# Opening the two fixed expert rounds of a mixture-of-experts layer by halves of the channels

## Chip, core and metric

The kernel runs on one NeuronCore of a Trainium2 chip. Its engines each work through a list of instructions of their own and wait for each other through semaphores: TensorE (PE; its weight loads are shown as PEld), VectorE (DVE), ScalarE (ACT), GpSimd (POOL) and SyncE (SP), which here only issues the transfers of weights. The metric is the device time of one execution in microseconds (us); lower is better.

## What is computed

A decoder trunk of two layers for 512 tokens of 1024 channels. Each layer has a token mixer (attention, gating unit, convolution), an output projection with layer norm, and a mixture of 32 experts of which each token uses two. The part that matters here is the experts:

```python
g_logit = xt @ wg + bg ; e_logit = xt @ we + be          # 4 groups, 8 experts in each
_, g_idx = lax.top_k(g_logit, 1)                         # one group,
top_logit, top_local = lax.top_k(e_logit_of_group, 2)    # two experts inside it
expert = g_idx * EXPERTS_PER_GROUP + top_local
...
def run_block(args):                                     # tokens of one expert
    rows, e = args
    xb = x_pad[rows]                                     # the gather
    hdn = jax.nn.silu(xb @ w_gate[e]) * (xb @ w_up[e])
    return hdn @ w_down[e]
...
out = segment_sum(y_rows[dest] * gate_sorted, tok_sorted)
x = layer_norm(ALPHA * x + out, ...)
```

All 32 experts are read in every layer: three matrices of 2 MB each, 6 MB per expert, 192 MB per layer in float32.

## The kernel before

**Rounds.** Each layer handles its experts in 13 rounds (`NR`). Rounds 0 and 1 (`FIXED`, `R0 = 2`) serve two experts each that are named in the program, so that their weights can be fetched before the router has decided; each of these experts has room for 64 tokens. Rounds 2 to 12 serve two or three experts each, chosen at run time: the experts are sorted by how many tokens they got, and the order (`self.ids`) is read by SP into registers that address the transfers. A round gathers its tokens (a product with a one-hot matrix), multiplies by the gate and up matrices (`first`, `hidden`, L1374), forms silu(gate) x up (`act`, L1386 and L1387), turns it (`turn`, L1393), multiplies by the down matrix (`second`, L1405), scales by the token's weight (`gated`) and adds the rows back to the tokens (`spread`, L1423).

**Gather.** `gather(quarters, n)` does a quarter of the channels at a time, two blocks `k` of 128 channels each. For each block eight matmuls add up: four 128-token blocks times a high part (`x1h`, fp32r) and a low part (`x1l`, f16). The moving operand is the one-hot matrix `oh` (in `fa`) or its f16 copy `oh16`, with 128 columns per round. `n=2` gathers for two rounds at once, so 256 columns. The result in a PSUM bank `t` is copied to `xg` (in the tile `f`) by ACT for the even block (L1345) and by DVE for the odd one (L1343); the DVE copy waits for the ACT copy.

**Weights.** Weight tiles of 1 MB (`w`) go into buffers from one free list (`self.free`). `feed` issues a transfer for each free buffer in the order of `self.queue`: all gate and up tiles of both fixed rounds (16), their eight down tiles, and then the tiles of the rounds chosen at run time. When the experts' part begins, the 16 gate and up tiles and one down tile are in place, and no buffer is free. A transfer therefore waits until the last product that reads the old tile in its buffer is done. SP issues strictly in order: a transfer that waits holds up all behind it. `hidden` with `parts=((0, 4), (4, 8))` does the gate products of channel blocks 0 to 3, the up products of 0 to 3, then gate and up of 4 to 7, so that the first half of the gate tiles comes free first.

**Order around the change.** PE, DVE, ACT, POOL and SP stand in written order here (`manual`). PE ends the router with six matmuls on the identity (`warm`, L1116) and then does: gather quarter 0, the sort's counting products (`sort_a`, L1213), gather quarter 1, the sort's table product (`sort_b`, L1226, which waits for four DVE operations L1221 to L1225), gather quarters 2 and 3, and then all gate and up products of round 0, with two `by_slot` transposes (L1356) in between and behind. DVE does the copies of the gather, the sort's few operations, the tokens' weights (`gating`, `gating_all`, `tokens`, L1249 to L1285), and the one-hots for rounds 2 and 3 (`gates`, L1306 to L1312).

Of the kernel before, what the change touches and what calls it, by code (L numbers as in the profile page):

```python
# [15 lines left out]
AF = mybir.ActivationFunctionType  # L16
# [149 lines left out]
class Trunk:  # L166
# [702 lines left out]
    def output(self, l):  # L869
# [118 lines left out]
        with self.manual(ET.PE):  # L988
# [31 lines left out]
            self.oh16 = f[:, 5, :].bitcast(F16).rearrange("p (a t s) -> p a t s", a=2, t=NT)  # L1020
            self.count_up()
            self.rank(NT - 1)
            self.places()
            self.warm(6)
            for r in range(R0):
                self.onehots(r)
            self.keys()
        self.give(wltag)
# [79 lines left out]
        nc.tensor.matmul(ps[:, 0:36], lt, self.two, start=False, stop=True)  # L1108
        nc.vector.tensor_copy(self.L[:, t, :], ps[:, 0:36])

    def warm(self, n):

        if n:
            ps = self.g()
        for _ in range(n):
            self.nc.tensor.matmul(ps[:, 0:128], self.ident, self.ident, start=True, stop=True)  # L1116

    def choose(self, tiles, more=()):

# [66 lines left out]
        ab, rk = self.ab[:, a:b, :], self.rk[:, a:b, :]  # L1186
        self.nc.vector.scalar_tensor_tensor(rk, ps, 1.0, ab, OP.add, OP.mult)

    def places(self):

        v = self.nc.vector
        self.ranks(NT - 1, NT)
        for r, (a, b) in enumerate(FIXED):
            le, on = (self.rt[:, c : c + 8].rearrange("p (t e) -> p t e", t=NT) for c in (384, 392))
            rk, u = self.rk[:, :, a : b + 1 : b - a], self.u[:, r, :]
            v.scalar_tensor_tensor(le, rk, 64.0, rk, OP.is_le, OP.mult)
            v.tensor_scalar(on[:, :, 0], le[:, :, 1], 0.0, 64.0, OP.is_gt, OP.mult)
            v.tensor_tensor(u, le[:, :, 0], le[:, :, 1], OP.add)
            v.tensor_tensor(u, u, on[:, :, 0], OP.add)


    def keys(self):
# [112 lines left out]
    def moe(self, l):  # L1315
# [5 lines left out]

        gain, bias = (lambda k, c=c: self.pp[:, c + k : c + k + 1] for c in (34, 42))

        def gather(quarters=range(4), n=2):

            w = 128 * n
            for kk in quarters:
                ps = self.t()
                for j in range(2):
                    k = 2 * kk + j  # L1330
                    i = 0
                    for src, one in ((x1h, oh), (x1l, self.oh16)):
                        for t in range(NT):
                            nc.tensor.matmul(  # L1334
                                ps[:, w * j : w * j + w], src[:, k, 128 * t : 128 * t + 128],
                                one[:, 0:n, t, :], start=(i == 0), stop=(i == 2 * NT - 1),
                            )
                            i += 1
                for j in range(2):
                    k = 2 * kk + j  # L1340
                    src = ps[:, w * j : w * j + w]
                    if j:
                        nc.vector.tensor_scalar(xg[:, k, 0:w], src, gain(k), bias(k), OP.mult, OP.add)  # L1343
                    else:
                        nc.scalar.activation(xg[:, k, 0:w], src, AF.Identity, bias=bias(k), scale=gain(k))  # L1345

        def gate_of(r):
            return self.sm.tile([128, 1], F32, tag="gv", name="gv")
# [16 lines left out]
        def weights(r, *names):  # L1365
            return [self.loaded[(l, n, r, e)] for n in names for e in range(members(r))]
# [179 lines left out]
        def release(r, *names):  # L1546
            for n in names:
                self.drop(*((l, n, r, e) for e in range(members(r))))

        def first(r, fill=(), keep=0):  # L1550

            pss = [self.g(), self.g()]
            xs = xg[:, :, 128 * (r % 2) : 128 * (r % 2) + 128]
            if r >= R0:
                for m, n in enumerate(("gate", "up")):
                    if m:
                        self.feed()
                    hidden(pss[m:], [weights(r, n)], xs, columns(ROUNDS[r - R0]), fill[4 * m : 4 * m + 4])
                    release(r, n)
            else:  # L1560
                w = [weights(r, n) for n in ("gate", "up")]
                hidden(pss, w, xs, halves, fill, ((0, 4), (4, 8)))
                release(r, "gate", "up")
            if keep == 1:
                spare.append(self.free.pop())
            held = [self.free.pop() for _ in range(4 if keep == 4 else 0)]
            self.feed()
            self.free.extend(held)
            return pss
# [22 lines left out]
        spare, row_steps = [], []  # L1592
        with self.manual(ET.PE, ET.SP):

            gather((0,))
            self.sort_a()
            gather((1,))
            self.sort_b()
            gather((2,))
            self.sort_c()  # L1600
            self.known = l
            self.feed()
            gather((3,))
            self.gating()
            self.gating_all()
            for r in range(R0):
# [2 lines left out]
                    in1=self.Gp[:, r, :].unsqueeze(2).broadcast_to([128, NT, 128]), op=OP.mult,  # L1609
                )  # L1610
            self.tokens()
            slots = []
            none = lambda: None
            pss = first(0, [none] * 5 + [lambda: slots.append(by_slot(0)), none, lambda: slots.append(by_slot(1))])
            h = act(pss)
            self.gates(2)
            self.gates(3)
            self.counts()
            nc.gpsimd.tensor_copy(self.cnt[:, 64:96], self.perm)
            pss = first(1, [none, lambda: turn(h, hT)])  # L1620
            self.fb = self.half("y", FR, "Y")[0]
            oT, gv = slots[0]
            steps = spreads(0, oT, second(0, gv))
# [228 lines left out]
```

## Time and profile before

| what | value |
|---|---|
| time, median of 3 runs | 1521.49 us (1520.38 to 1523.6) |
| the profiled execution | 1520.52 us; its span 1518.8 us |
| PE busy | 1368.6 us (90%) |
| DVE / ACT / POOL busy | 683.3 us (45%) / 397.2 us (26%) / 156.0 us (10%) |
| moved by DMA | 445.16 MB, mean 293 GB/s over the span |

The span is the stretch from the first to the last instruction in the trace; the execution's own time is 1.72 us longer. Busy shares are means over stages with different limits. The page's 40 slices show DMA at 410 to 419 GB/s in two long stretches, which are the experts' part of either layer, and between 1 and 56 GB/s just ahead of them. The experts' part of layer 0 begins at about 268 us of the span, that of layer 1 at about 1026 us.

### The profile page before, as it was taken

The numbers are of one execution on the slowest core, as the hardware profiler recorded it, in microseconds if no ns is written. First come the engines' busy times: TensorE is split into PE (matmuls) and PEld (weight loads), VectorE is DVE, ScalarE is ACT, GpSimd is POOL, SyncE is SP. The second block draws the span as 40 slices with busy tenths as digits, with TensorE's granted clock in tenths as the row PEclk, the third lists the DMA queues.
The fourth block names the chain that finished last, engine by engine and source line by source line (L and its number), as shares of the span: only waits on it lengthen the run. The fifth ranks groups of instructions, "written<-read, shape, count | busy, mean of one in ns | idle before, by whom it ended". The sixth has DMA issues, their size and how long they took to land. (4 is left out here: it accounts for less than half of the span.)

```text
span 1518.8 us, 22582 instructions
## 1 busy us (share of the span) xinstructions
PE 1368.6 (90%) x8828; PEld 750.3 (49%) x8829; DVE 683.3 (45%) x1528; ACT 397.2 (26%) x720; POOL 156.0 (10%) x190
## 2 busy tenths in 40 slices
PE   8999997999989898989699998979999898989894
PEld 7776576443434342434377665864434343433341
DVE  4347758534242424232553676585352424241325
ACT  5446544110101010101463555341101010101013
POOL 2112206000000000000141221060000000000001
PEclk9999999899999998999799998999999999999997
DMA  9410354499999999999911025444999999999994
GB/s 346 141 56 1 113 193 166 164 411 408 419 419 419 418 419 410 419 418 410 382 45 59 1 84 192 141 167 184 410 410 419 419 418 419 419 410 419 419 404 151
DMA packets 84551, 445.16 MB, mean 293 GB/s; under 512 B 8080, under 2 KB 14352, under 8 KB 36816
## 3 DMA queue, kind: packets, MB, share of 16 engines
q1 hardware_dynamic: 83184, 440.15, 72.2%
q0 software_dynamic: 960, 2.90, 0.6%
q8 instruction: 74, 1.21, 0.3%
q10 hardware_dynamic: 288, 0.52, 0.1%
q14 instruction: 45, 0.37, 0.1%
HBM read 441.45 MB, written 2.10 MB: 292 GB/s over the span
## 5 line engine op out<-in xcount | busy, mean ns | idle before, releaser
L1374 PE MATMUL g<-w,f 128*32 128x512 f32 (+1 forms) x3072 | 411.8, 602 | 36.3 <-DMA w<-expert_w_up 26.9
L1374 PEld LDWEIGHTS g<-w,f 128*32 128x32 f32 (+1 forms) x3072 | 113.6, 113 | 303.5 <-issue 220.6
L1405 PE MATMUL g<-w,f 128*32 128x512 f32 (+1 forms) x1536 | 215.4, 642 | 31.3 <-DMA w<-expert_w_down 15.6
L1405 PEld LDWEIGHTS g<-w,f 128*32 128x32 f32 (+1 forms) x1536 | 58.8, 118 | 165.0 <-issue 125.3
L1416 DVE SCALAR_TENSOR_TENSOR y<-g,gv,y 128x512 fp32r<-128x512 f32 x52 | 39.1, 751 | 208.8 <-ACT y L1415 206.4
L1428 DVE TENSOR_TENSOR X<-X,s 128x512 f32<-128x512 f32 x88 | 56.4, 683 | 127.1 <-PE s L1423 127.1
L1415 ACT ACTIVATE y<-g,gv 128x512 fp32r<-128x512 f32 x52 | 35.8, 689 | 245.0 <-PE g L1405 245.0
L1334 PE MATMUL t<-fa,mh 128*128 128x256 f32 (+1 forms) x448 | 82.8, 308 | 0.6 <-DVE f L1207 0.6
L1387 DVE TENSOR_TENSOR f<-g,f 128x512 f32<-128x512 f32 x26 | 17.9, 690 | 134.3 <-PE g L1374 130.9
L1345 ACT ACTIVATE f<-t,pp 128x256 f32<-128x256 f32 (+1 forms) x56 | 30.9, 551 | 177.1 <-PE t L1334 177.1
L1343 DVE TENSOR_SCALAR f<-t,pp 128x256 f32<-128x256 f32 (+1 forms) x56 | 29.4, 525 | 90.8 <-ACT f L1345 90.8
L1334 PEld LDWEIGHTS t<-fa,mh 128*128 128x128 f32 x448 | 62.7, 197 | 12.4 <-DVE X L1428 8.4
L1334 PE MATMUL t<-f,x1l 128*128 128x256 f16 (+1 forms) x448 | 67.5, 275 | 0.0
L1428 DVE TENSOR_TENSOR X<-X,t 128x512 f32<-128x512 f32 x88 | 56.3, 682 | 19.9 <-PE t L1423 19.9
L1423 PE MATMUL s<-y,fa 128*128 128x512 f32 x208 | 62.8, 422 | 2.4 <-ACT y L1415 1.8
L1386 ACT ACTIVATE f<-g 128x512 f32<-128x512 f32 x26 | 15.6, 598 | 188.3 <-PE g L1374 188.3
L1534 POOL DMA_DIRECT2D rows<-ln_gain x2 | 1.1, 550 | 586.9 <-PEq L1450 586.9
L1423 PEld LDWEIGHTS s<-y,fa 128*128 128x128 f32 x208 | 35.0, 188 | 51.2 <-issue 40.1
L1423 PE MATMUL t<-y,fa 128*128 128x512 f32 x208 | 59.1, 405 | 0.5 <-DVE xl L462 0.5
L1394 ACT COPY f<-s 128x512 f32<-128x512 f32 x26 | 15.2, 587 | 162.9 <-PE s L1393 135.1
L409 POOL TENSOR_TENSOR X<-X,E 128x512 f32<-128x512 f32 x11 | 16.3, 1486 | 332.5 <-ACT X L1712 168.8
L409 POOL TENSOR_TENSOR X<-X,f 128x512 f32<-128x512 f32 x32 | 40.9, 1309 | 87.8 <-DVE x1l L953 82.3
(343 smaller groups left out, 2273.8 us busy)
## 6 DMA issues: line engine op xcount, KB each, us to landing
w<-expert_w_gate SPq DMA_DIRECT2D x128, 1024.0 KB, 19.8
w<-expert_w_up SPq DMA_DIRECT2D x128, 1024.0 KB, 19.8
w<-expert_w_down SPq DMA_DIRECT2D x116, 1024.0 KB, 19.8
w<-w_in SPq DMA_DIRECT2D x20, 1024.0 KB, 13.9
w<-expert_w_down SPq DMA_DIRECT2D x48, 256.0 KB, 5.4
w<-w_out SPq DMA_DIRECT2D x8, 1024.0 KB, 5.5
X<-x SPq DMA_DIRECT2D x4, 512.0 KB, 5.8
w<-w_in SPq DMA_DIRECT2D x4, 512.0 KB, 8.1
```

The costliest lines, as they stand in the source:

```text
L409: e.tensor_tensor(out=x, in0=x, in1=row[:, 512 * h : 512 * h + 512], op=op)
L1334: nc.tensor.matmul(ps[:, w * j : w * j + w], src[:, k, 128 * t : 128 * t + 128], one[:, 0:n, t, :], start=(i == 0), stop=(i == 2 * NT - 1),)
L1343: nc.vector.tensor_scalar(xg[:, k, 0:w], src, gain(k), bias(k), OP.mult, OP.add)
L1345: nc.scalar.activation(xg[:, k, 0:w], src, AF.Identity, bias=bias(k), scale=gain(k))
L1374: nc.tensor.matmul(pss[m][a:b, :], xs[:, k, a:b], w[m][e][:, k, :], start=(k == 0), stop=(k == 7),)
L1386: nc.scalar.activation(hp, gate, AF.Silu)
L1387: nc.vector.tensor_mul(hp, up, hp)
L1405: nc.tensor.matmul(pss[hf][a:b, :], hT[:, 128 * j + a : 128 * j + b], part(e, hf, j), start=(j == 0), stop=(j == 3),)
L1415: nc.scalar.mul(yh, ps, gv)
L1416: nc.vector.scalar_tensor_tensor(yl, ps, gv, yh.bitcast(F32), OP.mult, OP.subtract)
L1423: nc.tensor.matmul(ps, oT[:, 128 * t : 128 * t + 128], y[q], start=(q == 0), stop=(q == 1))
L1428: nc.vector.tensor_add(x, x, ps)
```

## The change

Round 0 is begun with half of its channels. The first two quarters of the gather are done for round 0 alone (`gather((0, 1), 1)`, 128 columns), and its gate and up products over channel blocks 0 to 3 follow at once (`start(0, pss, low)`). Only then come `sort_a`, gather quarter 2 for both rounds, `sort_b`, gather quarter 3 and `sort_c`; then the products of round 0 over blocks 4 to 7. The first two quarters for round 1 are gathered separately behind that (`gather((0, 1), 1, 1)`), and round 1 is done by the same two halves. Both `by_slot` steps go from round 0 into the second half of round 1; on DVE `counts` goes ahead of `act`, and `gates(2)` and `gates(3)` fall behind the two `by_slot` steps. The six warming matmuls write into the bank `rp` that the router already holds instead of a bank of their own, behind `ranks`; `places` is done round by round between the one-hots. The `feed` behind `sort_c` goes; no buffer is free there in either kernel, and the transfers on SP's list keep their order.

```diff
-            self.places()
-            self.warm(6)
+            self.ranks(NT - 1, NT)
+            self.warm(6, self.rp[:, 384:512])
             for r in range(R0):
+                self.places(r)
                 self.onehots(r)
             self.keys()
...
-        def gather(quarters=range(4), n=2):
-
-            w = 128 * n
+        def gather(quarters=range(4), n=2, at=0):
+
+            w, to = 128 * n, slice(128 * at, 128 * (at + n))
...
-                                one[:, 0:n, t, :], start=(i == 0), stop=(i == 2 * NT - 1),
+                                one[:, at : at + n, t, :], start=(i == 0), stop=(i == 2 * NT - 1),
...
+        def start(r, pss, part, fill=()):
+
+            w = [weights(r, n) for n in ("gate", "up")]
+            hidden(pss, w, xg[:, :, 128 * r : 128 * r + 128], halves, fill, (part,))
+            if part[1] == 8:
+                release(r, "gate", "up")
+                self.feed()
...
-            gather((0,))
+            low, high = (0, 4), (4, 8)
+            gather((0, 1), 1)
+            pss = [self.g(), self.g()]
+            start(0, pss, low)
             self.sort_a()
-            gather((1,))
+            gather((2,))
             self.sort_b()
-            gather((2,))
+            gather((3,))
             self.sort_c()
             self.known = l
-            self.feed()
-            gather((3,))
             self.gating()
             self.gating_all()
...
             self.tokens()
+            self.counts()
+            start(0, pss, high)
+            h = act(pss)
+            gather((0, 1), 1, 1)
             slots = []
-            none = lambda: None
-            pss = first(0, [none] * 5 + [lambda: slots.append(by_slot(0)), none, lambda: slots.append(by_slot(1))])
-            h = act(pss)
+            pss = [self.g(), self.g()]
+            start(1, pss, low, [lambda: None, lambda: turn(h, hT)])
+            start(1, pss, high, [lambda r=r: slots.append(by_slot(r)) for r in range(R0)])
             self.gates(2)
             self.gates(3)
-            self.counts()
             nc.gpsimd.tensor_copy(self.cnt[:, 64:96], self.perm)
-            pss = first(1, [none, lambda: turn(h, hT)])
```

In the rows below, the changed kernel's lines are numbered one lower than before (L1333 for L1334, and so on). A product of the experts that the order counts once (L1374, L1405) is two rows in a trace.

PE from the end of round 0's products to the down products of round 0. Before (the first row is three quarters of round 0's products, L1356 is `by_slot`, L1393 `turn`, L1405 the down products):

```order
L1374 MATMUL g<-w,f 64x512 x24
L1356 MATMUL t<-ident,gt 128x128 x4
L1374 MATMUL g<-w,f 64x512 x8
L1356 MATMUL t<-ident,gt 128x128 x4
L1374 MATMUL g<-w,f 64x512 x8
L1393 MATMUL s<-ident,f 128x128 x4
L1374 MATMUL g<-w,f 64x512 x24
L1405 MATMUL g<-w,f 64x512 x16
```

After, from the last rows of round 1's own gather on:

```order
L1333 LDWEIGHTS x1l
L1333 MATMUL t<-f,x1l 128x128
L1373 MATMUL g<-w,f 64x512 x8
L1392 MATMUL s<-ident,f 128x128 x4
L1373 MATMUL g<-w,f 64x512 x12
L1355 MATMUL t<-ident,gt 128x128 x4
L1373 MATMUL g<-w,f 64x512 x4
L1355 MATMUL t<-ident,gt 128x128 x4
L1373 MATMUL g<-w,f 64x512 x8
L1404 MATMUL g<-w,f 64x512 x16
```

A gather with 128 columns now stands between the two rounds, and both `by_slot` steps stand in round 1. Round 0's products stand further up, 16 before the sort and 16 behind the gather's last quarter.

DVE around the sort. Before (L1343 are copies of the gather, L1221 to L1225 the operations for which PE's `sort_b` waits, L1231 and on `sort_c`):

```order
L1343 TENSOR_SCALAR f<-t,pp 128x256 x2
L1221 COPY f<-g 32x1
L1223 TENSOR_SCALAR f<-tab,f 32x32
L1224 TENSOR_SCALAR f<-g,tab 32x32
L1225 TENSOR_SCALAR f<-g,tab 32x32
L1343 TENSOR_SCALAR f<-t,pp 128x256
L1231 CAST ids<-g 128x32
```

After:

```order
L1342 TENSOR_SCALAR f<-t,pp 128x128 x2
L1342 TENSOR_SCALAR f<-t,pp 128x256
L1220 COPY f<-g 32x1
L1222 TENSOR_SCALAR f<-tab,f 32x32
L1223 TENSOR_SCALAR f<-g,tab 32x32
L1224 TENSOR_SCALAR f<-g,tab 32x32
L1342 TENSOR_SCALAR f<-t,pp 128x256
L1230 CAST ids<-g 128x32
```

The sort's operations still stand directly behind the copy of the gather quarter that PE does just ahead of `sort_b`: quarter 1 before, quarter 2 now.

DVE behind the tokens' weights. Before (L1358 and L1359 are `by_slot`, L1387 is `act`, L1306 to L1312 are `gates(2)`, and the same again `gates(3)`):

```order
L1285 TENSOR_TENSOR ur<-f,tab 128x88
L1358 TENSOR_SCALAR fa<-t 128x512
L1359 TENSOR_REDUCE gv<-t 128x1
L1358 TENSOR_SCALAR fa<-t 128x512
L1359 TENSOR_REDUCE gv<-t 128x1
L1387 TENSOR_TENSOR f<-g,f 128x512
L1306 TENSOR_SCALAR gt<-tab,ur,rs 128x128 x4
L1306 TENSOR_SCALAR f<-tab,ur,rs 128x128 x4
```

After:

```order
L1284 TENSOR_TENSOR ur<-f,tab 128x88
L1238 TENSOR_TENSOR f<-g,cap 128x32
L1239 CAST cnt<-f 128x32
L1240 TENSOR_REDUCE f<-f 128x1
L1241 CAST cnt<-f 128x1
L1386 TENSOR_TENSOR f<-g,f 128x512
L1342 TENSOR_SCALAR f<-t,pp 128x128 x2
L1357 TENSOR_SCALAR fa<-t 128x512
L1358 TENSOR_REDUCE gv<-t 128x1
L1357 TENSOR_SCALAR fa<-t 128x512
L1358 TENSOR_REDUCE gv<-t 128x1
L1305 TENSOR_SCALAR gt<-tab,ur,rs 128x128 x4
```

`act` and the copies of round 1's gather now stand ahead of `by_slot`, and `gates` still stands behind it, while `by_slot` itself has moved on PE into round 1.

## Rows read from the trace of the kernel before

**Rows 1.** Stages, PE only: stretch, length, PE busy, granted clock, DMA share, GB/s.
```profile
277.00:280.00 3.00, 3.00 (x16) 0.50 0.00 0
294.00:334.00 40.00, 40.00 (x216) 1.00 1.01 417
334.00:348.00 14.00, 14.00 (x98) 1.00 0.97 367
357.00:680.00 323.00, 290.24 (x2175) 0.96 1.01 418
...
1035.00:1038.00 3.00, 3.00 (x16) 0.50 0.00 0
1106.00:1440.00 334.00, 300.97 (x2260) 0.97 1.01 418
```
**Rows 2.** SP's waits from 282 to 345 us: total us, times, longest.
```profile
SPq L362 <- PE g L1374: 59.3, 8, 37.2
```
**Rows 3.** SP's waits from 345 to 690 us.
```profile
SPq L362 <- DMA w<-expert_w_down: 81.6, 41, 3.1
...
SPq L362 <- PE g L1374: 9.6, 13, 3.4
```
**Rows 4.** Timeline of PE, layer 0: start us, us, instruction, count, [idle before, releaser].
```profile
265.20 2.91 PE L1116 MATMUL g<-ident 128*128 128x128 f32 x12
268.39 1.19 PE L1334 MATMUL t<-fa,mh 128*128 128x256 f32 x4 [0.28 <-DVE f L1207]
...
272.99 0.61 PE L1334 MATMUL t<-f,x1l 128*128 128x256 f16 x4
275.98 0.46 PE L1226 MATMUL g<-f,ones 32*128 32x96 f32 x2 [2.39 <-DVE f L1225]
...
281.86 10.52 PE L1374 MATMUL g<-w,f 128*64 128x512 f32 x48
```
**Rows 5.** Timeline of DVE: the ranks, and the copy ahead of the sort.
```profile
265.40 0.19 DVE L1187 SCALAR_TENSOR_TENSOR rk<-g,f 128x32 f32<-128x32 f32 x1 [0.59 <-PE g L1173]
...
274.58 0.54 DVE L1343 TENSOR_SCALAR f<-t,pp 128x256 f32<-128x256 f32 x1 [2.01 <-ACT f L1345]
```
**Rows 6.** Timeline of PE: two gather quarters with 256 columns, then with 128.
```profile
318.55 0.74 PE L1334 MATMUL t<-fa,mh 128*128 128x256 f32 x4
...
322.38 0.60 PE L1393 MATMUL s<-ident,f 128*128 128x128 f32 x4
...
684.14 0.66 PE L1334 MATMUL t<-fa,mh 128*128 128x128 f32 x4
...
686.95 0.61 PE L1393 MATMUL s<-ident,f 128*128 128x128 f32 x4
```
**Rows 7.** Timeline of PE: `by_slot`, round 1's first products, round 0's down products.
```profile
292.31 0.66 PE L1356 MATMUL t<-ident,gt 128*128 128x128 f32 x4
...
297.06 3.65 PE L1374 MATMUL g<-w,f 128*64 128x512 f32 x16
...
311.58 7.04 PE L1405 MATMUL g<-w,f 128*64 128x512 f32 x32
```
**Rows 8.** Timeline of SP: issues of 1 MB tiles (from narrow stretches).
```profile
285.54 0.80 SPq L362 DMA_DIRECT2D w<-expert_w_down  x2
...
292.40 0.80 SPq L362 DMA_DIRECT2D w<-expert_w_down  x2
...
338.18 5.96 SPq L362 DMA_DIRECT2D w<-expert_w_down  x5
```
**Rows 9.** Timeline of DVE and ACT behind gather quarter 3: last copy, silu's table, `gates(2)`, `gates(3)`.
```profile
282.63 0.54 DVE L1343 TENSOR_SCALAR f<-t,pp 128x256 f32<-128x256 f32 x1 [1.38 <-ACT f L1345]
...
288.84 1.28 ACT L1386 ACT_TABLE_LOAD   x1 [5.24 <-DVE f L1283]
...
298.97 1.11 DVE L1306 TENSOR_SCALAR gt<-tab,ur,rs 128x128 f32<-128x128 f32 x4
...
302.55 1.11 DVE L1306 TENSOR_SCALAR gt<-tab,ur,rs 128x128 f32<-128x128 f32 x4
```

More of the change, by code (lines that the diff above doesn't have):

```diff
@@ L1109, in back, with warm @@
         nc.vector.tensor_copy(self.L[:, t, :], ps[:, 0:36])
-    def warm(self, n):
-        if n:
-            ps = self.g()
+    def warm(self, n, ps=None):
+        if ps is None and n:
+            ps = self.g()[:, 0:128]
         for _ in range(n):
-            self.nc.tensor.matmul(ps[:, 0:128], self.ident, self.ident, start=True, stop=True)
+            self.nc.tensor.matmul(ps, self.ident, self.ident, start=True, stop=True)
     def choose(self, tiles, more=()):
@@ L1187, in ranks, with places @@
         self.nc.vector.scalar_tensor_tensor(rk, ps, 1.0, ab, OP.add, OP.mult)
[L1189 to L1199, printed above, removed]
+    def places(self, r):
+        v, (a, b) = self.nc.vector, FIXED[r]
+        le, on = (self.rt[:, c : c + 8].rearrange("p (t e) -> p t e", t=NT) for c in (384, 392))
+        rk, u = self.rk[:, :, a : b + 1 : b - a], self.u[:, r, :]
+        v.scalar_tensor_tensor(le, rk, 64.0, rk, OP.is_le, OP.mult)
+        v.tensor_scalar(on[:, :, 0], le[:, :, 1], 0.0, 64.0, OP.is_gt, OP.mult)
+        v.tensor_tensor(u, le[:, :, 0], le[:, :, 1], OP.add)
+        v.tensor_tensor(u, u, on[:, :, 0], OP.add)
     def keys(self):
@@ L1342, in gather @@
                     if j:
-                        nc.vector.tensor_scalar(xg[:, k, 0:w], src, gain(k), bias(k), OP.mult, OP.add)
+                        nc.vector.tensor_scalar(xg[:, k, to], src, gain(k), bias(k), OP.mult, OP.add)
                     else:
-                        nc.scalar.activation(xg[:, k, 0:w], src, AF.Identity, bias=bias(k), scale=gain(k))
+                        nc.scalar.activation(xg[:, k, to], src, AF.Identity, bias=bias(k), scale=gain(k))
         def gate_of(r):
@@ L1553, in first @@
             xs = xg[:, :, 128 * (r % 2) : 128 * (r % 2) + 128]
-            if r >= R0:
-                for m, n in enumerate(("gate", "up")):
-                    if m:
-                        self.feed()
[L1558 to L1563, printed above, removed]
+            for m, n in enumerate(("gate", "up")):
+                if m:
+                    self.feed()
+                hidden(pss[m:], [weights(r, n)], xs, columns(ROUNDS[r - R0]), fill[4 * m : 4 * m + 4])
+                release(r, n)
             if keep == 1:
@@ L1593, in moe @@
         with self.manual(ET.PE, ET.SP):
-            gather((0,))
+            low, high = (0, 4), (4, 8)
+            gather((0, 1), 1)
+            pss = [self.g(), self.g()]
+            start(0, pss, low)
             self.sort_a()
-            gather((1,))
+            gather((2,))
             self.sort_b()
-            gather((2,))
+            gather((3,))
             self.sort_c()
             self.known = l
-            self.feed()
-            gather((3,))
             self.gating()
```

## The prediction

> **What bounds the kernel now.** I read the stages first, then who waits for whom on the queue that issues the weights, then the order of time around the change. In the stages [rows 1] two facts stand side by side. From 294 to 334 us and from 334 to 348 us PE is busy for the whole stretch, and in the second of them the transfers drop from 417 to 367 GB/s: the stream of weights runs short while PE never stops. From 357 to 680 us it is the other way round: 418 GB/s without a dip, and PE is busy for only 290.24 of 323 us. The waits of the issuing queue say the same. Between 282 and 345 us SP waits for PE, 59.3 us for gate and up products alone [rows 2]; from 345 us on it waits for earlier transfers, 81.6 us for down tiles alone against 9.6 us for the gate and up products [rows 3]. So the layer has two parts. Up to about 345 us PE's list of work sets when buffers come free; after that the stream sets the time, and a stream that starts its unbroken part later by some time ends later by the same time. Layer 1 shows the same unbroken part, 418 GB/s from 1106 to 1440 us [rows 1].
>
> The last issues that PE holds back are the tiles at 338.18 us [rows 8], behind the down products of round 1. The question for the change is therefore not when the first buffer comes free, but when PE gets through both fixed rounds.
>
> PE's path ahead of them [rows 4]: the gather starts at 268.39, waits 2.39 us for the sort's operations on DVE before 275.98, and the fixed products begin at 281.86; round 1's begin at 297.06 and round 0's down products at 311.58 [rows 7]. Behind the wait for the sort the granted clock is 0.50 from 277 to 280 us, the 1.2 GHz level, with PE busy throughout; the same comes in layer 1 from 1035 to 1038 us [rows 1].
>
> **The change part by part.** A product in the program's order is two rows of the trace, so 24 of the order are the 48 rows that take 10.52 us [rows 4]; 3.51 us for 16 rows.
>
> *The split gather.* Two quarters with 256 columns take from 318.55 to 322.38, 3.83 us; two quarters with 128 columns from 684.14 to 686.95, 2.81 us [rows 6]. Half the columns cost 73%, not 50%. Before, quarters 0 and 1 are done once (3.83 us); after, twice (5.62 us). That adds 1.79 us to PE in each layer, on the path: PE has no idle time up to 348 us into which it could fall.
>
> *The warming matmuls.* They now write into the bank that `ranks` reads, and follow it: `ranks` ends at 265.40 + 0.19 = 265.59 [rows 5], against a start at 265.20 before. They take 2.91 us, so they end at 268.50, and the gather, which needs only round 0's one-hot by then, can follow. It started at 268.39 [rows 4]: 0.1 us later. Bounds 0 and 0.4 us, since the 0.28 us of idle before the gather may go or stay.
>
> *The products of the two rounds* are as many as before, and so are the `by_slot` transposes (0.66 us each [rows 7]), which go from round 0 to round 1: nothing by the time that round 1 ends.
>
> *The wait for the sort* stays. Before, the sort's DVE operations stand behind the copy at 274.58, which waits for ACT's copy of the same quarter [rows 5], and PE's table product follows at 275.98. After, they stand behind the copy of quarter 2, just ahead of the table product again. The same 2.39 us, only some 8 us later, with 16 products done ahead of it. Cost: nothing. What is queued behind it on PE is quarter 3 and then the second half of round 0.
>
> *The copies for round 1.* This wait is new. ACT has to copy the first block of round 1's gather behind its silu, and silu's table is loaded only when DVE is through `tokens`: the load begins at 288.84 and ends at 290.12 [rows 9], that is 8.26 us after PE's gather ended at 281.86 [rows 4]. Behind it come silu and the copy, each put at the 0.54 us of the last gather copy [rows 9], and three small operations of `sort_c` now stand in the chain, 0.3 us together (an estimate from the 0.19 us of `ranks`, part of which overlaps). So the first block is there some 9.6 us after PE has ended gather quarter 3, and PE needs it after 32 product rows and a gather, 7.02 + 2.81 = 9.83 us. It fits by 0.2 us, estimated. I take 0, and bound it by 0 and 1 us per layer.
>
> *The gates.* `gates(2)` and `gates(3)` take 302.55 - 298.97 = 3.58 us each [rows 9] and now start behind the second `by_slot`. Round 1's products begin at 297.06 - 1.3 (two `by_slot` fewer ahead) + 1.9 = 297.7, and that `by_slot` ends behind 48 product rows, the turn and itself at about 310; with two DVE operations (put at 0.54 us each) and 7.16 us of gates it is 318.3. PE needs them for the next gather at 318.55 + 1.9 = 320.5. They fit by 2 us: nothing, and where that cover is gone each microsecond counts in full.
>
> *The transfers.* The two tiles issued at 285.54 go out when the first half of the gate products is done, now about 10 us earlier. The next four wait for the second half: 292.40 [rows 8] less 1.02 us (3.83 - 2.81, one gather of round 1 not yet done) plus 0.1, so 0.9 us earlier. From round 1 on each release is 1.9 us later. An early tile is worth nothing where the stream runs short afterwards anyway, and it does between 334 and 348 us [rows 1]: one meets the same release at 338.18, now 1.9 us later.
>
> Sum: 1.79 + 0.1 = 1.9 us per layer, 3.8 us for two layers. The profiled execution took 1520.52 us and would take 1524.3; the median of the three runs, 1521.49, becomes 1525.3.
>
> **The rivals.** *The clock holds behind the sort's wait.* From 275.98 to 281.86 PE did the table product (0.46 us) and two quarters, 5.88 us against 0.46 + 3.83 at the 2.4 GHz level: 1.6 us lost [rows 4, 6]. If the clock did not fall in the changed kernel, 0.3 us per layer would remain of the 1.9: 1522.1. For it: the wait now lies behind a long busy stretch. Against it: before the wait at 275.98 PE had also been busy, the clock fell all the same, in both layers. The Trainium skill ("TensorE: Matmul & The Clock Gate", section "Why this matters for your kernels") asks only that longer pauses between bursts be avoided, and lets a pause as short as this pass; by it this rival would be the forecast. The trace disagrees with it here, with 0.50 granted behind a pause of 2.39 us.
>
> *The stream's head start counts* (faster). If the stream, and not PE, set the pace from the first release on, each layer would end earlier by the lead of the four tiles, 0.9 us, or 0.9 + 1.6 = 2.5 us where the clock holds too: 1519.7 or 1516.5. It decides if the transfers no longer run short between 334 and 348 us. Against it: PE is busy without a gap there, and SP waits for it.
>
> *The new wait binds* (slower still). If ACT's copy for round 1 comes late, PE stands before round 1's first product, and each 0.5 us costs 1 us in all. At 0.5 to 1 us per layer the time is 1526.3 to 1527.3. It decides as soon as the chain behind gather quarter 3 exceeds 9.83 us.
>
> *The change does nothing for the end*: the stream absorbs the 1.9 us. That would need spare time at the release of 338.18, where the transfers are already short. 1521.5.
>
> **How the numbers follow.** About 0.2% (3 us) is what a measurement of this kernel can tell from no change; slower begins at 1524.5. The forecast has 0.60, of which a fifth falls below 1524.5, since its sum may be 1 us off either way. The held clock has 0.16 (no change), the new wait 0.13 (slower), the head start 0.09 (0.05 of it faster, 0.04 no change), the absorbed delay 0.02. Slower: 0.48 + 0.13 = 0.61. No change: 0.12 + 0.16 + 0.04 + 0.02 = 0.34. Faster: 0.05. The range goes from 1519.5, which takes in the held clock and the small head start, to 1528.0 above the new wait; outside are the large head start and sums of several bounds.
>
> **What would show it.** In the changed profile: the first two tiles issued near 276 us and the next four near 291.5; the transfers empty in between; gathers of 128 columns at 2.8 us for two quarters; round 0's down products at 313.5 instead of 311.58; the transfers short again between 334 and 350 us with PE fully busy; the unbroken stream beginning 1.9 us later. Down products of round 0 at or before 311.6 would refute the sum; an unbroken stream from about 293 us on would refute the claim that PE sets the pace; idle time on PE ahead of round 1's first product would show the new wait.

## The result, and the profile of the changed kernel

The changed kernel is slower, by half a per cent: 1531.2 us (1526.1 to 1532.3, 6 runs) against 1522.2 us for the kernel before, a ratio of 1.0051 with a 95% interval of 1.0033 to 1.0069. Two later comparisons gave 1527.6 against 1521.3 us (1.0040, 1.0027 to 1.0052) and 1528.5 against 1522.3 us (1.0037, 1.0021 to 1.0053). So the forecast of 1525.3 us had the direction right and the size too small: the first median lies 3.2 us above the end of the range, the later two at it.

The profiled execution of the changed kernel has a span of 1529.4 us, 10.6 us more than before. First the stages that answer to [rows 1], PE only (stretch, length, PE busy, granted clock, DMA share, GB/s):

```profile
289.00:292.00 3.00, 3.00 (x15) 0.53 0.00 0
294.00:334.00 40.00, 40.00 (x238) 1.00 0.93 374
334.00:348.00 14.00, 14.00 (x78) 1.00 0.86 332
357.00:680.00 323.00, 289.16 (x2184) 0.97 1.01 418
1050.00:1053.00 3.00, 3.00 (x15) 0.50 0.00 0
1106.00:1440.00 334.00, 300.91 (x2270) 0.97 1.01 416
```

The picture is the old one, later: PE without a gap up to 348 us while the transfers run short (374 and 332 GB/s, 417 and 367 before), then the unbroken stream. The slow clock behind the sort's wait is still there in both layers. SP's waits from 282 to 345 us (total, times, longest), as [rows 2]:

```profile
SPq L362 <- PE g L1373: 28.9, 4, 14.6
SPq L362 <- PE g L1404: 22.0, 4, 12.8
```

and from 345 to 690 us, as [rows 3]:

```profile
SPq L362 <- DMA w<-expert_w_down: 77.0, 39, 2.6
...
SPq L362 <- PE g L1373: 13.2, 15, 3.7
```

SP still waits for PE first and for the stream afterwards. PE around the change in layer 0 (start, length, instruction, count, [idle before, releaser]), for [rows 4, 7]:

```profile
263.66 2.03 PE L1117 MATMUL g<-ident 128*128 128x128 f32 x16
...
270.67 2.93 PE L1117 MATMUL g<-ident 128*128 128x128 f32 x12 [0.28 <-DVE rk L1188]
273.25 1.09 PE L1333 MATMUL t<-fa,mh 128*128 128x128 f32 x4
...
276.85 7.09 PE L1373 MATMUL g<-w,f 128*64 128x512 f32 x32
...
288.31 0.66 PE L1225 MATMUL g<-f,ones 32*128 32x96 f32 x2 [2.09 <-DVE f L1224]
288.90 1.22 PE L1333 MATMUL t<-fa,mh 128*128 128x256 f32 x4
...
292.29 7.09 PE L1373 MATMUL g<-w,f 128*64 128x512 f32 x32
299.31 0.66 PE L1333 MATMUL t<-fa,mh 128*128 128x128 f32 x4
...
302.21 3.65 PE L1373 MATMUL g<-w,f 128*64 128x512 f32 x16
...
318.20 7.04 PE L1404 MATMUL g<-w,f 128*64 128x512 f32 x32
```

The second gather of quarters 0 and 1 is there (299.31 to 302.21). Round 1's first products follow it with no idle time, and so does everything up to the down products at 318.20. But the first row shows something that the prediction does not mention. The last eight warming matmuls of the router start at 263.66; before, they started here:

```profile
258.62 2.03 PE L1116 MATMUL g<-ident 128*128 128x128 f32 x16
```

That is 5.04 us later, *ahead of* the first instruction that the change touches: up to there PE does the same products in the same order in both traces. To separate the two effects I cut each profile at the same events: these warming matmuls (W), round 0's down products (D), the last round's `turn` (T), and the next layer's first product. "Lead" is from the start to W in layer 0, "fixed" from W to D, "stream" from D to T, "end" from T to the next layer's first product (in layer 1: to the end), "mixer" from that product to W of layer 1. All in us, each the difference of two starts (fixed, before: 311.58 [rows 7] - 258.62 = 52.96).

| profile | lead | fixed 0 | stream 0 | end 0 | mixer 1 | fixed 1 | stream 1 | end 1 | span |
|---|---|---|---|---|---|---|---|---|---|
| before | 258.62 | 52.96 | 414.84 | 19.28 | 270.85 | 52.57 | 414.77 | 34.91 | 1518.8 |
| before_again | 259.11 | 52.90 | 414.37 | 19.43 | 271.69 | 52.32 | 414.49 | 34.89 | 1519.2 |
| before_third | 260.75 | 52.81 | 414.82 | 19.22 | 271.03 | 52.46 | 415.22 | 34.59 | 1520.9 |
| changed | 263.66 | 54.54 | 414.36 | 20.44 | 271.56 | 54.67 | 414.01 | 36.16 | 1529.4 |
| after_again | 258.79 | 54.63 | 414.29 | 20.54 | 271.99 | 54.50 | 416.68 | 34.58 | 1526.0 |
| after_third | 261.18 | 55.80 | 414.80 | 19.15 | 270.87 | 54.58 | 415.27 | 35.55 | 1527.2 |
| split_only | 258.78 | 53.69 | 415.32 | 20.55 | 272.21 | 54.90 | 415.45 | 34.80 | 1525.7 |
| one_gather | 259.15 | 51.35 | 414.97 | 20.24 | 271.85 | 51.03 | 415.35 | 35.36 | 1519.3 |
| no_sort_wait | 260.58 | 48.62 | 414.45 | 20.04 | 271.67 | 48.38 | 414.63 | 34.93 | 1513.3 |
| sort_ahead | 258.96 | 50.89 | 414.95 | 20.55 | 272.09 | 50.54 | 414.41 | 36.11 | 1518.5 |
| whole_sort_ahead | 258.23 | 48.81 | 415.06 | 19.32 | 270.85 | 48.95 | 414.60 | 35.38 | 1511.2 |
| delay | 259.21 | 54.87 | 414.62 | 20.22 | 271.57 | 54.52 | 414.70 | 35.79 | 1525.5 |
| warm_wait | 261.75 | 52.51 | 414.89 | 19.13 | 272.04 | 50.38 | 414.13 | 35.87 | 1520.7 |
| warm_tail | 260.50 | 48.41 | 414.56 | 17.75 | 273.59 | 48.42 | 414.57 | 33.20 | 1511.0 |

Means of the three profiles of either kernel: the two fixed stretches together 105.3 before and 109.6 after, +4.2 us; the two streams 829.5 and 829.8, +0.3; lead, ends and mixer together 584.8 and 588.2, +3.4. The sum is the difference of the mean spans, 1519.6 and 1527.5. Of the +3.4, 1.7 lie in the lead, 1.4 in the ends and 0.3 in the mixer.

The traces also show what the scatter outside the changed code is made of. Added up over lead, ends and mixer, PE was busy while the granted clock was 0.50 for 40.3, 45.4 and 46.4 us in the three profiles before, and for 56.3, 45.0 and 47.9 us in those of the changed kernel. Over all 14 profiles, a straight line through the points gives 0.48 us more in the lead for each microsecond of such time, and 0.47 and 0.48 us in the ends of the two layers; the mixer follows less closely (0.33). At 0.48 the 16.0 us more in the first profile of the changed kernel than in the first one before are worth 7.7 us, and these parts are 8.2 us longer. The fixed stretches hold about equally much of it in both kernels, 7.8 to 8.4 us before and 8.0 to 8.3 us changed, except for 10.2 us in layer 0 of `after_third`. So their growth is not the clock's, but for about 1 us in that one stretch.

### The profile page after: what moved, and what is told of

Its sections match the earlier page's. It is cut to its first block, busy times and chain, and to the rows that moved or that the text cites. A ratio compares the mean times of both kernels' runs of the same rounds, so it can differ in the third digit from the quotient of the medians.

```text
span 1529.4 us, 22722 instructions
## 1 busy us (share of the span) xinstructions
PE 1376.6 (90%) x8892; PEld 756.7 (49%) x8893; DVE 685.6 (45%) x1532; ACT 397.4 (26%) x724; POOL 155.8 (10%) x190
## 5 line engine op out<-in xcount | busy, mean ns | idle before, releaser
L1333 PE MATMUL t<-fa,mh 128*128 128x256 f32 (+1 forms) x480 | 87.6, 306 | 0.0
L1333 PEld LDWEIGHTS t<-fa,mh 128*128 128x128 f32 x480 | 67.2, 198 | 12.8 <-DVE X L1427 8.4
L1333 PE MATMUL t<-f,x1l 128*128 128x256 f16 (+1 forms) x480 | 68.2, 266 | 0.0
L1427 DVE TENSOR_TENSOR X<-X,t 128x512 f32<-128x512 f32 x88 | 56.3, 681 | 22.1 <-PE t L1422 22.1
L1393 ACT COPY f<-s 128x512 f32<-128x512 f32 x26 | 15.2, 584 | 148.7 <-PE s L1392 148.7
```

What stands on the lines that cost most here:

```text
L1333: nc.tensor.matmul(ps[:, w * j : w * j + w], src[:, k, 128 * t : 128 * t + 128], one[:, at : at + n, t, :], start=(i == 0), stop=(i == 2 * ...
L1427: nc.vector.tensor_add(x, x, ps)
```

## The experiments

**The same kernels again.** No edit.

> The changed kernel once more, beside the kernel before on the same chip. Theory A (PE's list: the split gather adds 1.9 us per layer, and the other 5 us of the first measurement lie in layer 0's token mixer, whose code is the same, where the granted clock fell for longer): the times scatter between about 1526 and 1532, and the profile's fixed rounds are 1.6 to 2.3 us per layer longer than before whatever the total. Theory B (the change itself costs 9 us): the times stay within 1 us of 1531, and the fixed rounds take 4 to 5 us more per layer.

> A third profile of the changed kernel, for where its executions differ. Theory A: 54.5 to 54.7 us from the router's last eight warming matmuls to round 0's down products in both layers, whatever the execution takes in all; the rest of its time varies with the stretches in which the granted clock is 0.50 in the token mixers and at the layer's end. Time about 1527.7, 5.8 us above before; 3.7 of them are the two fixed stretches.

> The unchanged kernel once more, for a second profile of it. In the first one the stretch from the last eight warming matmuls of the router to round 0's down products took 52.96 and 52.57 us in the two layers; the changed kernel took 54.5 to 54.7 in both of its profiles. Theory A (the split costs 1.6 to 2.1 us there, and what came on top lies in other stretches that scatter from one execution to the next): 52.6 to 53.0 us again, and the other stretches 1 to 4 us longer in sum than in the first profile, which was among the shortest executions. Theory B (the change also lengthens the other stretches): the others as in the first profile, within 1 us in sum. Time against the kernel before: ratio 1.000 by both.

> A third profile of the kernel before: 52.3 to 53.0 us in the same stretch in both layers. If the shorter end of layer 0 (19.3 us from the last turn on) and the shorter approach to layer 1's router in the first two profiles were chance, they are as often long as short, here too; if they belong to the kernel, they are short again and the time is 1520 to 1522.

Measured: 1527.64 and 1528.54 us for the changed kernel, 1522.65 and 1521.76 us for the one before (ratios 1.0002, 0.9989 to 1.0015, and 0.9993, 0.9983 to 1.0004). The first profile's 5 us in the lead came back as 0.2 and 2.6 us in the other two, against 0.5 and 2.1 us for the kernel before: the lead scatters, and on the recorded profile it was at its worst. The single executions scatter as well, from 1519.7 to 1529.2 us before and from 1524.7 to 1532.6 us changed. The fixed stretches do not, but for one: `after_third` has 55.80 in layer 0, where 54.5 to 54.7 was expected.

Two expectations did not come out for theory A alone. Outside the fixed stretches `before_again` is only 0.7 us longer than the first profile, which is what theory B said. And the end of layer 0 was short in `before_third` too (19.22 us), so by that expectation the short end belongs to the kernel before; of the changed kernel's three, one is as short.

What the lead did in the recorded profile shows in the clock. PE in two stretches of layer 0's token mixer, in the kernel before:

```profile
176.00:178.00 2.00, 1.49 (x10) 1.00 0.80 336
...
200.00:206.00 6.00, 6.00 (x35) 1.00 0.78 273
```

and in the changed kernel:

```profile
176.00:178.00 2.00, 1.95 (x10) 0.50 0.59 250
...
200.00:206.00 6.00, 6.00 (x20) 0.50 0.51 175
```

PE is busy throughout from 200 to 206 us in both, with 35 rows done at the 2.4 GHz level and 20 at the 1.2 GHz level. Just ahead of it PE waits for ACT, in the kernel before:

```profile
197.53 0.50 PE L889 MATMUL g<-fa,mh 128*128 128x512 f32 x1 [0.74 <-ACT E L743]
```

and in the changed one:

```profile
199.43 0.59 PE L889 MATMUL g<-fa,mh 128*128 128x512 f32 x1 [1.85 <-ACT E L743]
```

1.1 us more of idle time was followed by 6 us at half the clock. None of the changed code has run by then.

**The split alone.** Quarters 0 and 1 are gathered for each round apart, at the old place; the rest is the kernel before.

```diff
-            gather((0,))
+            gather((0,), 1)
+            gather((0,), 1, 1)
...
-            gather((1,))
+            gather((1,), 1)
+            gather((1,), 1, 1)
```

> The kernel before, with gather quarters 0 and 1 done for round 0 and round 1 separately (128 columns each) at the place where they stood; no products are moved. Theory A (the second gather is the cost): 1.8 us per layer more, about 1526, as in the changed kernel where its mixer is undisturbed. If the moved products, the moved by_slot steps or the early release were the cost, this kernel would stay at 1522.

Measured: 1527.49 us against 1521.32 (1.0028, 1.0010 to 1.0046). The fixed stretches are 53.69 and 54.90 us, 0.8 and 2.5 above the mean before; the layer 1 stretch contains 5 us at half the clock behind the sort's wait (granted 0.50 from 1039 to 1044 us, PE busy for all of it), which layer 0 has for a shorter time. The mean, 1.6 us per layer, is near what was expected, but this run does not give the split's price: PE is busy at half the clock for 19.9 us in the two fixed stretches, 3.6 us more than the mean before, which at 0.48 is worth 1.7 of the 3.2 us, and the sort's wait is shorter here, 1.81 us.

**The new order with the old gather.**

```diff
-            gather((0, 1), 1)
+            gather((0, 1))
...
-            gather((0, 1), 1, 1)
```

> The changed kernel with its first two gather quarters done for both rounds at once (256 columns), and without the second gather before round 1; products, sort and releases stay in the new order. Theory A: 1.8 us per layer less than the changed kernel, so 1522 to 1523, no different from before. If the early release of the first two tiles were worth something, up to 1 us per layer below before, 1520. If the new order were the cost, 1526 or more.

Measured: 1520.92 us against 1521.32 (1.0002, 0.9988 to 1.0015). Without the split the kernel is as fast as before, and 6.7 us faster than the changed kernel beside it (1527.64). But the split is not all that differs. The fixed stretches, 51.35 and 51.03 us, are 3.6 us per layer shorter than the changed kernel's, twice the price of the split, and 1.5 us shorter than before. PE at the sort's wait in `one_gather`:

```profile
285.19 0.46 PE L1225 MATMUL g<-f,ones 32*128 32x96 f32 x2 [2.10 <-DVE f L1224]
285.58 0.74 PE L1333 MATMUL t<-fa,mh 128*128 128x256 f32 x4
```

and its clock behind the wait in both layers:

```profile
285.00:288.00 3.00, 2.81 (x20) 1.00 0.00 0
1043.00:1046.00 3.00, 2.71 (x20) 1.00 0.00 0
```

The wait is as long as in the changed kernel (2.10 and 2.09 us), the 32 product rows ahead of it are the same, and the clock does not fall; the four rows behind it take 0.74 us, against 1.22 at 288.90 in the changed kernel. This is the rival "the clock holds" with about its price (1.6 us). It came true in this kernel and not in the one it was made for. So this pair does not separate the split from the clock. Nor do the 3.0 us that the fixed stretches gain against before show in the time: lead, ends and mixer are 586.6 us, 1.8 more than the mean before, and the streams 0.8 more.

**No wait for the sort.** The table product of the sort goes behind all gathers; the DVE operations stay where they are. `sort_mm` is that product, taken out of `sort_b`.

```diff
...
             self.sort_b()
             gather((2,))
+            gather((3,))
+            self.sort_mm()
             self.sort_c()
             self.known = l
             self.feed()
-            gather((3,))
```

> The kernel before, with the sort's table product moved on PE behind gather quarters 2 and 3, so that PE does not wait for DVE there; nothing else moves. Theory A (PE's list sets when the unbroken stream begins): the wait of 2.4 us goes, and with it the 1.6 us lost at half the clock behind it, so up to 4 us per layer: 1514 to 1517. If the stream of weights set the time from the first release on, the first release would still come 4 us earlier and the result would be the same; if neither did, 1522.

Measured: 1514.32 us against 1521.32 (0.9949, 0.9933 to 0.9964). The fixed stretches are 48.62 and 48.38 us, 4.2 us less per layer. The wait of 2.39 and 2.11 us is a good half of that; the rest, 1.9 us, is the slow clock behind it, which is gone (granted 1.00 from 273 to 282 us). The table product no longer waits:

```profile
279.09 0.46 PE L1229 MATMUL g<-f,ones 32*128 32x96 f32 x2
```

This kernel is faster than both.

**The split without the wait.** In the changed kernel the sort goes right behind the first gather and its table product behind round 0's first 16 products; then the same with the split undone as in `one_gather`.

```diff
...
             gather((0, 1), 1)
+            self.sort_a()
+            self.sort_b()
             pss = [self.g(), self.g()]
             start(0, pss, low)
-            self.sort_a()
+            self.sort_mm()
             gather((2,))
-            self.sort_b()
             gather((3,))
```

> The changed kernel, with the sort's counting products and its DVE operations put between the first half gather and round 0's first sixteen products, and the table product behind those. PE then has 7.0 us of products while DVE works, so the wait of 2.1 us goes, and if the fall of the clock is a consequence of that wait, the 1.7 us of slow clock behind it go too. The split gather stays. Theory A (the cost of the split is PE's list, 1.8 us in each layer, and passes to the end): the stretch from the router's last eight warming matmuls to round 0's down products is 54.6 - 3.8 = 50.8 us, 2.3 us more than in the kernel without the sort's wait and without the split (48.5), and the time 1514.3 + 3.7 = 1518. If the clock falls for another reason: 52.5 us and 1521.5. Theory B (the split costs several us elsewhere too): 1520 or more with a stretch of 50.8.

> The kernel with the sort's operations ahead of round 0's first products, but with the first two gather quarters done once for both rounds (256 columns) and the second gather of these quarters left out: the split is undone and nothing else. There is no sort's wait in either, so the clock has no pause to fall behind. Theory A (the split costs PE's list 1.8 us in each layer): the stretch from the router's last eight warming matmuls to round 0's down products goes from 50.9 and 50.5 us to 49.1 and 48.7, and the time from 1520.9 to 1517.2. If the split costs more than its own products, down to 1514.3, the time of the kernel of before without the sort's wait. If it costs nothing once the wait is gone: 1520.9.

Measured: 1520.87 us with the split (0.9988, 0.9977 to 1.0000), 1513.78 us without (0.995, 0.9933 to 0.9966). The table product in layer 0 of the two, one after the other:

```profile
279.64 0.46 PE L1228 MATMUL g<-f,ones 32*128 32x96 f32 x2
...
279.88 0.46 PE L1228 MATMUL g<-f,ones 32*128 32x96 f32 x2
```

It does not wait for the sort in either, so this pair has the split's price without a fall of the clock behind that wait: 50.89 and 50.54 us against 48.81 and 48.95, that is 2.1 and 1.6 us, 1.84 on the mean. The prediction's term was 1.79. But the medians are 7.1 us apart, twice that, and both times came out as the rival lines of the two expectations had it: 1520 or more with a stretch of 50.8, and down to 1514.3. How far that holds is less sure. The two were measured apart, the second in 4 runs, and by their ratios to the kernel before they are 5.8 us apart, with intervals of 1.8 and 2.5 us either way. In the two profiles the other half stands in the ends of the layers (20.55 and 36.11 against 19.32 and 35.38), in the mixer (272.09 against 270.85) and in the lead, at places where both kernels do the same work. There PE is busy at half the clock for 50.5 us with the split and 41.9 us without; at 0.48 the difference is worth 4.1 us, and these parts differ by 3.9 us.

**A pure delay.** Eight matmuls on the identity behind round 1's products in the kernel before.

```diff
...
             pss = first(1, [none, lambda: turn(h, hT)])
+            self.warm(8, self.s())
```

> The kernel before, with eight matmuls on the identity behind round 1's gate and up products, ahead of round 0's down products: PE loses 2.0 us in each layer at the place where the changed kernel is late, by work that touches no gather, no wait and no clock. Theory A (PE's list sets the time there and the stream cannot make it up): 2.0 us later at the end of each layer, 1525.4. The stream absorbs it (the rival with a chance of 0.02): 1521.4. Theory B (a delay there costs more than itself): above 1527.

Measured: 1527.33 us against 1522.31 (1.0045, 1.0026 to 1.0063), 5.0 us for 2 x 2.0 us put in. The rows, and no idle time behind them:

```profile
312.10 2.05 PE L1116 MATMUL s<-ident 128*128 128x128 f32 x16
314.08 7.09 PE L1405 MATMUL g<-w,f 128*64 128x512 f32 x32
```

The fixed stretches grow by 2.0 and 2.1 us over the mean before, and the streams behind them are as long as ever (414.62 and 414.70): the delay passes to the end of each layer one to one. The time lies just above 1527, where the expectation had theory B, but the interval (4.0 to 9.6 us) takes in the 4.1 us of the fixed stretches, and lead, ends and mixer are 586.8 us, 2.0 above the mean before, with 48.3 us of PE at half the clock. The rival by which the stream absorbs it falls, and the head start falls with it: in 14 profiles, with fixed stretches of 48.4 to 55.8 us, 27 of the 28 streams lie between 414.0 and 415.5 us.

**PE busy in the wait.** Nine matmuls on the identity ahead of the sort's table product in the kernel before; the wait itself stays.

```diff
...
             gather((1,))
+            self.warm(9, self.t())
             self.sort_b()
```

> The kernel before, with nine matmuls on the identity (about 2.2 us of PE work on nothing) ahead of the sort's table product, so that PE is busy while it waits; the wait itself stays as long. Tells the pause from the length of the path. If the fall of the granted clock to 0.50 follows from the pause: no stretch at 0.50 behind the table product, the two gather quarters behind it in 3.8 instead of 5.5 us, 1.6 us less in each layer, 1518. If the clock falls there whatever PE does: the stretch at 0.50 stays and the time is 1521.5, or up to 0.4 us more for warming matmuls that outlast the wait.

Measured: 1521.25 us against 1522.31 (0.9990, 0.9978 to 1.0002), so the time did not tell. The trace did. PE at the sort's wait in layer 1:

```profile
1034.39 2.17 PE L1116 MATMUL t<-ident 128*128 128x128 f32 x18
1036.66 0.46 PE L1226 MATMUL g<-f,ones 32*128 32x96 f32 x2
1037.04 0.74 PE L1334 MATMUL t<-fa,mh 128*128 128x256 f32 x4
```

The clock in layer 0 ahead of the wait, behind it, and behind it in layer 1:

```profile
271.50:275.00 3.50, 3.48 (x16) 0.50 0.02 5
281.00:284.00 3.00, 3.00 (x28) 1.00 0.00 0
...
1037.00:1040.00 3.00, 3.00 (x27) 1.00 0.00 0
```

Behind the covered wait the clock is 1.00 in both layers, and layer 1's fixed stretch is 50.38 us, 2.1 less. In layer 0 the first gather quarters ran at half the clock (the first row), behind a wait of 1.09 us for their one-hot that was 0.28 us before [rows 4], and that took most of the gain: 52.51 us. In that layer, what was won at one pause was lost at the one ahead of it. Lead, ends and mixer, 588.8 us, took the rest.

**PE busy at the layer's end.** In `no_sort_wait`, warming matmuls around the last round's `turn`.

```diff
...
+                if last:
+                    self.warm(7, self.s())
                 turn(h, hT)
+                if last:
+                    self.warm(2, self.s())
```

> The kernel of before without the sort's wait, with seven warming matmuls (1.8 us) ahead of the last round's turn and two behind it, where PE stands idle for 1.90 and 0.73 us at the end of each layer. From the turn to the next layer's first product it took 19.3 and 19.4 us in the two profiles of the kernel before, and 20.0 to 20.6 us in six others, all with the turn at 1.12 instead of 0.66 us and the down products behind it longer. If that difference is the clock falling behind these pauses: the turn at 0.66 us, 19.3 us or less again, and 1513.3 to 1514.0 in all (0.3 to 1 us less than without the warming). If not: 20.0 us and 1514.3, or 0.3 us more for warming matmuls that outlast a wait.

Measured: 1511.44 us against 1522.27 (0.9924, 0.9908 to 0.9941), the lowest median here and 2 us below what was expected. The end of layer 0 in the kernel before:

```profile
726.42 0.66 PE L1393 MATMUL s<-ident,f 128*128 128x128 f32 x4 [1.90 <-DVE f L1387]
727.81 6.89 PE L1405 MATMUL g<-w,f 128*32 128x512 f32 x48 [0.73 <-ACT f L1394]
```

in the changed kernel:

```profile
732.56 1.11 PE L1392 MATMUL s<-ident,f 128*128 128x128 f32 x4 [1.90 <-DVE f L1386]
734.41 7.60 PE L1404 MATMUL g<-w,f 128*32 128x512 f32 x48 [0.73 <-ACT f L1393]
```

and in this one:

```profile
723.47 0.66 PE L1396 MATMUL s<-ident,f 128*128 128x128 f32 x4
723.96 0.61 PE L1116 MATMUL s<-ident 128*128 128x128 f32 x4
724.86 5.36 PE L1408 MATMUL g<-w,f 128*32 128x512 f32 x48 [0.28 <-ACT f L1397]
```

The same 48 rows take 5.36 us where PE had one pause of 0.28 us, and 6.89 and 7.60 us where it had two, of 1.90 and 0.73 us. Ends of 17.75 and 33.20 us are the shortest of all; the two groups that the others form, 19.1 to 19.4 and 20.0 to 20.6 us for layer 0, both contain slow clock: PE is busy at 0.50 there for 2.8 to 3.4 us in the short ones and 4.9 to 5.9 us in the long ones, and not at all in `warm_tail`. Part of the gain is given back: the mixer behind it takes 273.59 us, 1.9 more than in `no_sort_wait`, with 33.8 instead of 28.0 us of PE at half the clock. That the ends differ by the clock is shown; why the kernel before had the short one in three of three profiles and the changed kernel in one of three is not.

## Why the prediction was wrong, step by step

**What bounds the kernel** was right. PE's list carries the fixed rounds, the stream carries the rest, and a delay of PE there arrives at the end undiminished (`delay`, and the stream columns).

**The split gather** was right: 1.79 us predicted, 1.84 measured in the pair without the sort's wait, and the second gather is 2.90 us from 299.31 to 302.21 where 2.81 was taken. **Warming, `by_slot`, copies for round 1 and gates** cost nothing beyond the sum, as said: the gather starts 9.59 us behind the router's last eight warming matmuls, where it started 9.77 us behind them; no idle time stands before round 1's products at 302.21, nor before the gather of 256 columns behind the down products. **The transfers** moved as said: tiles issued at 280.53 and 295.97 us, which less the 4.86 us that the gather started late is 275.7 and 291.1, against the 276 and 291.5 predicted.

**The sort's wait** was put at an unchanged 2.39 us with an unchanged slow stretch. The wait is 2.09 us now, and the clock fell behind it in both layers of all three profiles, so the sum held: the fixed stretches grew by 2.1 us per layer on the mean of three profiles, 1.9 predicted. But the ground given for it was too simple, and that it held here is in part luck. The prediction argued from the old wait, behind which the clock fell, that it falls behind the new one. `one_gather` has 2.10 us and stays at the 2.4 GHz level, the changed kernel has 2.09 us and falls to the 1.2 GHz level. The wait's length alone does not say which; with PE kept busy in the wait the clock did not fall behind it (`warm_wait`, both layers). The Trainium skill ("TensorE: Matmul & The Clock Gate", section "Why this matters for your kernels") lets a pause as short as this pass. The trace of `one_gather` agrees with that (1.00 granted behind 2.10 us), the one of the changed kernel does not (0.50 behind 2.09 us).

**The step that failed** is the last one of the sum: "The profiled execution took 1520.52 us and would take 1524.3; the median ... becomes 1525.3", with a range made of bounds inside the changed code only. It took the rest of the kernel to be constant. It is not: lead, ends and mixer came to between 583.7 and 591.8 us in the three profiles of either kernel, at places of the same work, and the time of PE at half the clock there goes from 40.3 to 56.3 us. The first profile of the kernel before was the shortest in this sum (583.7 us), that of the changed kernel the longest (591.8): of the 10.6 us between the two spans 8.2 are here, 3.7 in the fixed stretches, and -1.2 in the streams. That the two recorded profiles were the extremes is chance; that the range had no room for it is the error.

Taken over three profiles, +4.2 us lies in the changed code and +3.4 us outside it. That second part is no work that the change adds, and the streams do not carry it (+0.3 us). For the most part it is the clock: on the mean 5.7 us more of PE at half the clock, worth 2.7 us at 0.48. Whether the change brings this about is open. For it speaks that the end of layer 0 is short in three of three profiles before and in one of three changed, and that the pair `sort_ahead` and `whole_sort_ahead` differs there too. Against it speaks that half of the 3.4 us lies in the lead, ahead of all changed code; that `one_gather` and the changed kernel differ by 6.7 us in the medians and by 7.2 us in the fixed stretches, which leaves nothing for the other parts; and that a longer end of layer 0 stands in `one_gather`, `no_sort_wait` and `delay` too, which have no split. The intervals do not decide it: those of the two later comparisons (4.1 to 7.9 and 3.2 to 8.1 us) take in 4.2 us, the first one (5.0 to 10.5 us) does not. Where the clock falls depends on what came before, and a shift by a few us may move it. That is my reading; which shift gives which pattern was not settled.

**The rivals.** The clock's hold (0.16) did not happen here, though it did in `one_gather`; the head start (0.09), the new wait (0.13) and the absorbed delay (0.02) are all refuted by rows. The chance for slower (0.61) was on the right side.

## What to carry to other kernels

- A gather whose cost lies in fixed parts (half the columns for 73% of the time) did not pay when it was split to start something earlier, since what waits was paced by the engine that does the splitting. The sort's wait, which the new order left in place, could be hidden by moving one matmul (`no_sort_wait`: -7.0 us).
- Where a wait of 2.1 to 2.4 us on TensorE was followed by a stretch at half the granted clock, its price was about double its length here. Other useful work in it was worth most; matmuls on nothing were worth something, and the next wait then has to be looked at too.
- Ahead of a forecast, cut the kernel into stretches and ask how much each scatters from one execution to the next. One profile can't tell, and a range from the changed code alone was too narrow here. Behind it, add up in each stretch how long PE was busy at half the clock: about half of the difference was here the part that the change's own work does not explain.

## What the runs showed of the hardware

- Behind pauses of nearly the same length (2.09 to 2.10 us), with the same 32 product rows and gather quarter 2 ahead, the granted clock fell to 0.50 in the changed kernel and stayed at 1.00 in `one_gather`, in both layers of each. In the token mixer a pause of 1.85 us was followed by 0.50 for 6 us and one of 0.74 us was not.
- How long the clock stays low varies: the table product and gather quarter 3 behind the sort's wait ran at 0.50 throughout in layer 0 of `after_third` (285.45 to 290.00 us), and the 32 product rows behind them took 8.26 instead of 7.09 us.
- Over 14 profiles, each microsecond that PE was busy at 0.50 went with 0.47 to 0.48 us more in the lead and in the ends of the layers; it ranged from 6.5 to 16.5 us in the lead and from 0.0 to 6.1 us in the ends.
- A PE delay of 2.0 us ahead of a stream at 418 GB/s came out of 415 us of stream unchanged within 0.5 us.
